# Strassen-Winograd weights on Trainium2: product P7's weights by subtraction from the running sum

## The chip, the cores and the metric

The kernel runs on one core of one Trainium2 chip. The metric is the device time of one execution in microseconds (us), the median of several runs. A profiled execution of the same program gives the page and the trace. In the trace PE is the matrix engine (TensorE), DVE is VectorE, ACT is ScalarE, POOL is GpSimd and SP is SyncE.

## The reference

One layer of a transformer-like block, batch 1, 512 tokens, width 2048, all in float32. A combined input projection feeds two token mixers, grouped-query attention and a Fourier mixing. Each is multiplied by a SiLU gate and projected to 2048 channels. The two are merged with sigmoid gates, and one output projection feeds a gated residual and a final norm:

```
g_a = sigmoid(p_rest[..., R_GA:R_GB]);  g_b = sigmoid(p_rest[..., R_GB:])
y_a = (attn * silu(z_a)) @ w_pa
y_b = (fourier_mix(u_b) * silu(z_b)) @ w_pb
return (g_a * y_a + g_b * y_b) @ w_o
```

The change touches how the weights of `g_a`, `g_b` (2048 x 4096 together) and `w_o` (2048 x 2048) are prepared.

## The kernel before

**Products.** These two products are computed in six groups: groups 0 to 3 for the gates, then the branch projections, then groups 4 and 5 for `w_o`. A group is a 2x2 block product in the form of Strassen and Winograd: seven products instead of eight. Each takes one form of the activations and one combination of the four weight blocks (0,0), (0,1), (1,0), (1,1). `PRODUCTS` (line 49 on) names them. P1 takes block (0,0); Q5 takes (0,0) + (0,1); Q6 adds (1,1) to that, and Q4 adds (1,0). P2 takes (1,0), Q3 takes (1,1), and P7 takes (0,1) + (1,1). The orders are `ONE_GROUP` (P1, Q5, P2, Q6, P7, Q3, Q4; groups 0 to 3 and 5) and `OUT_GROUP` (P1, P2, Q5, Q6, P7, Q3, Q4; group 4).

**Pieces.** Each product comes in four pieces, with a weight tile of 128x1024 (512 KB) each. A piece is multiplied by 12 matmuls of 128x512: two column tiles, two token tiles, and three passes each (`mm3`, lines 258 to 260: high part by high part, high by low, low by high). `split_from` (lines 133 and 134) makes the two parts of a weight tile: ScalarE copies the rounded high part `whi`, VectorE subtracts it to get the low part `wlo`.

**The running sum.** Four tiles R, one for each piece (`chain`), hold the sum that P1, Q5, Q6 and Q4 use one after the other. SyncE loads block (0,0) into R for P1 (line 172). In groups 0 to 3 Q5's block is loaded as a raw tile and added by VectorE (line 205). Every other block is added by an accumulating DMA from GpSimd's queue (line 214), issued in the order of the code right after the split of the stage before.

**Raw tiles.** Blocks that don't go into R are loaded by SyncE (line 169) into raw slots: eight in groups 0 to 3, six in groups 4 and 5. `x` and other inputs take the same slots. A load is issued in the order of `todo`, when a slot has come free. P7 takes two raw tiles for a piece, and VectorE adds them (line 205) before the split. `get` splits several pieces ahead of the one that is multiplied: five in groups 0 to 3, four in groups 4 and 5.

**Order.** All engines work through their instructions in the order that the build's scheduler has written. VectorE also makes the sums of the products (lines 830, 876, 1204, 1205 and others), ScalarE moves finished products and computes the sigmoids. After the last product the two token tiles of the last quarter are normalized and stored, one after the other (lines 1222 to 1261).

Of the kernel before, what the change touches and what calls it, by code (L numbers as in the profile page):

```python
# [13 lines left out]
ALU = mybir.AluOpType  # L14
# [29 lines left out]

FORMS = ("Z5", "S2", "S3", "S4")
CHAIN = ((0, 0), (0, 1), (1, 1), (1, 0))
PRODUCTS = (("P1", "A11", 0, "a"), ("Q5", "Z5", 1, "b"), ("P2", "A12", ((1, 0),), "a"), ("Q6", "S2", 2, "b"),
            ("P7", "S3", ((0, 1), (1, 1)), "c"), ("Q3", "S4", ((1, 1),), "b"), ("Q4", "A22", 3, "c"))  # L50
ONE_GROUP = ("P1", "Q5", "P2", "Q6", "P7", "Q3", "Q4")
OUT_GROUP = ("P1", "P2", "Q5", "Q6", "P7", "Q3", "Q4")

# [32 lines left out]
def block_kernel(ctx, tc, xT, ctxT, x, c_row, w_ss, w_gate, vecs, qkg, rope, dft_c, dft_s,  # L86
                 w_start, w_kv, w_m, w_g, w_pab, w_o, final_g, out):
    nc = tc.nc
# [8 lines left out]
    wp = sb("wp")  # L97
# [14 lines left out]
    def uid(s):  # L112
        cnt[0] += 1
        return f"{s}{cnt[0]}"
# [14 lines left out]
    def bank2():  # L129
        return ps.tile([P, 1024], F32, tag="b2", bufs=2, name=uid("pd"))  # L130

    def split_from(src, hi, lo):
        nc.scalar.activation(hi, src, ACT.Copy)  # L133
        nc.vector.tensor_tensor(lo, src, hi.bitcast(F32), op=ALU.subtract)  # L134
# [3 lines left out]
    chain, left = [], [0] * 4  # L138
    raw_pools, hl_pools = [(wp, RAW, "raw", RAW)], [wp] * HL

    class Piece:
# [1 line left out]

        def __init__(self, key, parts, cols, n, kind="wp", stage=None, pc=0, nxt=None, dst=None):
            self.key, self.parts, self.cols, self.n, self.kind = key, parts, cols, n, kind
            self.stage, self.pc, self.nxt, self.dst = stage, pc, nxt, dst
            self.raws, self.out, self.aside = [], None, False

    def stream(key, src, *a, **k):
        todo.append(Piece(key, src if isinstance(src, list) else [src], *a, **k))
# [37 lines left out]
    def hl_tiles():  # L190
        hl_pools.append(hl_pools.pop(0))
        pool = hl_pools[-1]
        if isinstance(pool, tuple):
            return [slot_tile(p, (1024,), F32R) for p in pool]
        if isinstance(pool, int):
            return [Halves([pairs[2 * pool + k][i][:, :, 256:] for k in range(2)]) for i in range(2)]
        return [pool.tile([P, 1024], F32R, tag=t, bufs=hl_pools.count(pool), name=uid("w" + t)) for t in ("hi", "lo")]

    def split_piece(e):
        if e.out is not None or e.kind == "raw":  # L200
            return
        raws = [r for _, r in e.raws]
        src = raws.pop(0) if e.stage is None else chain[e.pc]
        for r in raws:
            nc.vector.tensor_tensor(src, src, r, op=ALU.add)  # L205
        hi, lo = e.dst() if e.dst else hl_tiles()
        if isinstance(hi, Halves):
            for k in range(2):
                split_from(src[:, 512 * k : 512 * k + 512].rearrange("p (a c) -> p a c", a=2), hi.parts[k], lo.parts[k])
        else:  # L210
            hi, lo = hi[:, : e.cols], lo[:, : e.cols]
            split_from(src, hi, lo)
        if e.nxt is not None:
            nc.gpsimd.dma_start(src, e.nxt, accum_op=ALU.add)
        if e.stage == 3:
            left[e.pc] = 0
        r = lambda t: t if isinstance(t, Halves) else t.rearrange("p (n m) -> p n m", n=e.n)
        e.out = (r(hi), r(lo))

    def get(key):  # L220
        load_more()
        turn = [e for e in ahead if not e.aside]
        assert turn[0].key == key, (turn[0].key, key)
        for e in turn[: len(hl_pools)]:
            split_piece(e)
        load_more()
        e = turn[0]
        ahead.remove(e)
        free.extend(p[0::2] for p, _ in e.raws if p in retired)
        return e.raws[0][1] if e.kind == "raw" else e.out  # L230
# [12 lines left out]
    def slot_tile(p, shape, dt):  # L243
        return p[0].tile([P] + list(shape), dt, tag=p[1], bufs=1, name=uid("s"))
# [70 lines left out]
    def stream_product(name, g, w, by_dve):  # L315

        what = next(p[2] for p in PRODUCTS if p[0] == name)
        for pc in range(4):
            key = (name, g, pc)
            if isinstance(what, tuple):  # L320
                stream(key, [w[a, b, pc] for a, b in what], 1024, 2)
            else:
                part = lambda i: w[CHAIN[i][0], CHAIN[i][1], pc]
                stream(key, [part(what)] if what in by_dve else [], 1024, 2, stage=what, pc=pc,
                       nxt=part(what + 1) if what < 3 and what + 1 not in by_dve else None)
                todo[-1].first = part(0)

    flat = lambda v: v.rearrange("p t c -> p (t c)")
# [7 lines left out]
    for g in range(4):  # L336
        for name in ONE_GROUP:
            stream_product(name, g, w_g[g], BY_DVE_GATES)
            if g == 0 and name in LOADED:
                todo.extend(lambda f=f, h=h: load_form(f, h) for f in LOADED[name] for h in range(2))  # L340
            if g >= 2 and name in DONE:
                half, c = DONE[name]
                stream(("yb", half, 2 * (g % 2) + c), flat(yb_d[half, 2 * (g % 2) + c]), 1024, 2, "raw")
# [7 lines left out]
    for name in OUT_GROUP:  # L351
        stream_product(name, 4, w_o[1], BY_DVE_OUT)
        if name in DONE:
            half, c = DONE[name]
            stream(("x", half, 2 + c), flat(x[half, 2 + c]), 1024, 1, "raw")
    for name in ONE_GROUP:
        stream_product(name, 5, w_o[0], BY_DVE_OUT)
        half, c = {"P2": (0, 0), "P7": (1, 1), "Q3": (1, 0)}.get(name, (0, 0))
        if name == "Q3":
            stream(("x", 0, 1), flat(x[0, 1]), 1024, 1, "raw")  # L360
            todo.insert(len(todo) - 5, todo.pop())
        if name in ("P2", "P7", "Q3"):
            stream(("x", half, c), flat(x[half, c]), 1024, 1, "raw")
# [4 lines left out]
    part = ppool.tile([P, NS - 2, T], F32, name="part")  # L368
# [313 lines left out]
    for which, half in ((0, 0), (0, 1), (1, 1)):  # L682
        toks = range(3 * half, 3 * half + 3) if which == 0 else (4, 5)
        b = bank2()
        accs = [b[:, :512], b[:, 512:], bank()]
        for pc in range(8):
# [9 lines left out]
            if keys and pc in (1, 3, 5):  # L696
                a, t = keys.pop(0)
# [3 lines left out]
        for a, t in zip(accs, toks):  # L701
            a = a.rearrange("p (h d) -> p h d", h=4)
# [213 lines left out]
    def load_form(f, h, q=None):  # L916
        if (f, h) not in whole:
            return False
        i = FORMS.index(f)
        (q or nc.sync).dma_start(whole[f, h], f_d[i, :, 4 * h : 4 * h + 4, :])  # L920
# [128 lines left out]

    for i, f in enumerate(FORMS):  # L1050
        forms[f] = [None] * 8
# [33 lines left out]

    raws, merged, mf, comb = {}, {}, {n: [None] * 8 for n in ("A11", "A12", "A22") + FORMS}, {}
    held = {}
# [282 lines left out]
```

## Time and profile before

| | |
|---|---|
| median of 3 runs | 1386.93 us (1384.67 to 1387.5) |
| profiled execution | 1383.63 us |
| its span, first to last instruction | 1381.9 us |
| mean granted TensorE clock | 0.994 |
| PE busy | 1348.6 us (98%) |
| DVE, ACT, POOL busy | 911.2 us (66%), 629.7 us (46%), 113.7 us (8%) |
| HBM read | 257.34 MB |
| group 0 | from 757.4 us |
| groups 1, 2, 3 | from 839.4, 915.5, 991.7 us |
| branch projections | from 1067.8 us |
| groups 4, 5 | from 1204.4, 1284.7 us |
| last matmul | 1369.5 us |

A row of a timeline has the start in us from the start of the span, the duration in us, the engine, the line, the operation, output <- inputs by the program's names with buffer numbers left out, and in brackets the engine's idle time before it with what ended it. `wr` is a raw tile, `R` the running sum, `x` and `y` are accumulators of products. Busy time is an average over stages with different limits; what a change in one stage is worth is read from that stage.

### The profile page before, as it was taken

To read this page: it belongs to the slowest core of one execution; us is meant where nothing else is said; L and a number is where in the kernel's file an instruction comes from. 1 tells how busy PE (TensorE), PEld (TensorE's weight loads), DVE (VectorE), ACT (ScalarE), POOL (GpSimd) and SP (SyncE) were. 2 spreads that over 40 slices of the span, in tenths; PEclk is the share of its full clock that TensorE was granted. 3 is DMA by queue.
4 is the path that set the end of the run, shared out by engine and by line. 5 is a ranking of instruction groups with operands and counts; after the bars stand their busy time and mean duration, and the time that the engine had idled before them with its cause. 6 is when DMAs were issued, how large, how long until landed. Compare 5 with 4: busy or idle time off the path is not lost. (4 is left out here: it accounts for less than half of the span.)

```text
span 1381.9 us, 17609 instructions
## 1 busy us (share of the span) xinstructions
PE 1348.6 (98%) x6810; PEld 1105.2 (80%) x6810; DVE 911.2 (66%) x1191; ACT 629.7 (46%) x861; POOL 113.7 (8%) x167
## 2 busy tenths in 40 slices
PE   7999999999999999999999899999999999999986
PEld 4667789888888888888887688888888888878865
DVE  5765596767866658756743776665956546477577
ACT  5322253534545445455544655453544224364534
POOL 0110000011100001000000100100010100020100
PEclk9999999999999999999999999999999999999998
DMA  9887453635453334433446998888898854488973
GB/s 384 333 349 264 164 187 104 190 122 185 147 152 108 121 116 148 149 100 114 130 142 242 348 300 246 249 228 253 274 275 297 315 153 138 132 190 272 237 222 130
DMA packets 76115, 283.67 MB, mean 205 GB/s; under 512 B 8704, under 2 KB 9344, under 8 KB 71680
## 3 DMA queue, kind: packets, MB, share of 16 engines
q1 hardware_dynamic: 53712, 188.42, 40.6%
q0 software_dynamic: 17136, 76.56, 20.6%
q10 hardware_dynamic: 5184, 17.57, 3.3%
q8 instruction: 53, 0.87, 0.3%
q14 instruction: 30, 0.25, 0.1%
HBM read 257.34 MB, written 25.17 MB: 204 GB/s over the span
## 5 line engine op out<-in xcount | busy, mean ns | idle before, releaser
L133 ACT ACTIVATE whi<-wr 128x1024 fp32r<-128x1024 f32 x178 | 185.2, 1044 | 295.8 <-PE pb L259 83.6
L134 DVE TENSOR_TENSOR wlo<-wr,whi 128x1024 fp32r<-128x1024 f32 x178 | 213.7, 1204 | 143.2 <-ACT whi L133 143.0
L258 PE MATMUL pb<-s,whi 128*128 128x512 f32 x512 | 206.7, 405 | 1.3 <-ACT s L424 1.3
L259 PE MATMUL pb<-s,whi 128*128 128x512 f32 x512 | 200.7, 392 | 0.1
L260 PE MATMUL pb<-s,wlo 128*128 128x512 f32 x512 | 200.4, 392 | 0.0
L259 PE MATMUL y<-wlo,s 128*128 128x512 f32 x320 | 126.7, 396 | 7.1 <-DVE wlo L134 7.0
L259 PE MATMUL x<-wlo,s 128*128 128x512 f32 x324 | 126.7, 391 | 1.5 <-DVE wlo L134 1.5
L258 PE MATMUL x<-whi,s 128*128 128x512 f32 x324 | 126.7, 391 | 1.3 <-ACT s L836 1.1
L258 PE MATMUL y<-whi,s 128*128 128x512 f32 x320 | 126.1, 394 | 0.2 <-ACT s L833 0.2
L260 PE MATMUL x<-whi,s 128*128 128x512 f32 x324 | 126.3, 390 | 0.0
L260 PE MATMUL y<-whi,s 128*128 128x512 f32 x320 | 125.7, 393 | 0.0
L258 PEld LDWEIGHTS pb<-s,whi 128*128 128x128 f32 x512 | 96.1, 188 | 22.4 <-issue 3.7
L260 PEld LDWEIGHTS pb<-s,wlo 128*128 128x128 f32 x512 | 96.1, 188 | 21.1 <-issue 0.4
L259 PEld LDWEIGHTS pb<-s,whi 128*128 128x128 f32 x512 | 96.4, 188 | 17.1 <-DVE s L425 1.0
L133 ACT ACTIVATE whi<-R 128x1024 fp32r<-128x1024 f32 x66 | 69.7, 1059 | 64.6 <-PE x L260 39.4
L134 DVE TENSOR_TENSOR wlo<-R,whi 128x1024 fp32r<-128x1024 f32 x66 | 80.1, 1220 | 17.1 <-ACT whi L133 17.1
L973 ACT ACTIVATE p<-pd,mx 128x768 f32<-128x768 f32 x48 | 43.2, 899 | 87.3 <-DVE mx L971 87.3
L259 PEld LDWEIGHTS y<-wlo,s 128*128 128x128 f32 x320 | 60.7, 190 | 22.4 <-DVE wlo L134 9.9
L259 PEld LDWEIGHTS x<-wlo,s 128*128 128x128 f32 x324 | 60.8, 188 | 15.5 <-DVE wlo L134 3.1
L258 PEld LDWEIGHTS x<-whi,s 128*128 128x128 f32 x324 | 60.8, 188 | 14.7 <-ACT s L836 1.5
L258 PEld LDWEIGHTS y<-whi,s 128*128 128x128 f32 x320 | 60.7, 190 | 13.4 <-ACT s L833 0.5
L260 PEld LDWEIGHTS y<-whi,s 128*128 128x128 f32 x320 | 60.8, 190 | 12.7
(270 smaller groups left out, 2662.1 us busy)
## 6 DMA issues: line engine op xcount, KB each, us to landing
wr<-in_w_g SPq DMA_DIRECT2D x80, 512.0 KB, 7.9
wa<-in_w_ss POOLq DMA_DIRECT2D x28, 1024.0 KB, 8.2
wr<-in_w_m SPq DMA_DIRECT2D x44, 512.0 KB, 3.7
wr<-in_w_gate SPq DMA_DIRECT2D x32, 512.0 KB, 3.7
wr<-in_w_pab SPq DMA_DIRECT2D x32, 512.0 KB, 4.4
R<-in_w_g POOLq DMA_DIRECT2D x32, 512.0 KB, 9.6
wr<-in_w_o SPq DMA_DIRECT2D x32, 512.0 KB, 5.0
wr<-in_w_start SPq DMA_DIRECT2D x26, 512.0 KB, 7.1
```

The source lines that it names most:

```text
L133: nc.scalar.activation(hi, src, ACT.Copy)
L134: nc.vector.tensor_tensor(lo, src, hi.bitcast(F32), op=ALU.subtract)
L258: nc.tensor.matmul(o, ah, bh, start=start, stop=False, skip_group_check=cont)
L259: nc.tensor.matmul(o, ah, bl, start=False, stop=False, skip_group_check=cont)
L260: nc.tensor.matmul(o, al, bh, start=False, stop=stop, skip_group_check=cont)
L973: nc.scalar.activation(p, sc[:, :NKEY], ACT.Exp, bias=mx[:, 0:1], accum_out=mx[:, 1:2])
```

## The change

P7 now loads block (0,0) as its only raw tile, and VectorE subtracts it from the running sum of three: R - (0,0) = (0,1) + (1,1). The accumulation of the fourth block (1,0) into R was issued behind Q6's split. It is now issued behind P7's piece, because the subtract reads R as well. In all, 24 loads of 512 KB go; the number of VectorE instructions stays. In the changed file most lines stand one to four lines further down: the split is at 134 and 135, the gates' add at 206, the new subtract at 208, the loads at 170 and 173, the accumulating DMA at 217.

```diff
-            ("P7", "S3", ((0, 1), (1, 1)), "c"), ("Q3", "S4", ((1, 1),), "b"), ("Q4", "A22", 3, "c"))
+            ("P7", "S3", ((0, 0),), "c"), ("Q3", "S4", ((1, 1),), "b"), ("Q4", "A22", 3, "c"))
...
         for r in raws:
             nc.vector.tensor_tensor(src, src, r, op=ALU.add)
+        if e.off:
+            nc.vector.tensor_tensor(src, chain[e.pc], src, op=ALU.subtract)
         hi, lo = e.dst() if e.dst else hl_tiles()
...
         if e.nxt is not None:
-            nc.gpsimd.dma_start(src, e.nxt, accum_op=ALU.add)
+            nc.gpsimd.dma_start(chain[e.pc], e.nxt, accum_op=ALU.add)
...
+            part = lambda i: w[CHAIN[i][0], CHAIN[i][1], pc]
             if isinstance(what, tuple):
-                stream(key, [w[a, b, pc] for a, b in what], 1024, 2)
+                off = name == "P7"
+                stream(key, [w[a, b, pc] for a, b in what], 1024, 2, pc=pc, nxt=part(3) if off else None, off=off)
             else:
-                part = lambda i: w[CHAIN[i][0], CHAIN[i][1], pc]
                 stream(key, [part(what)] if what in by_dve else [], 1024, 2, stage=what, pc=pc,
-                       nxt=part(what + 1) if what < 3 and what + 1 not in by_dve else None)
+                       nxt=part(what + 1) if what < 2 and what + 1 not in by_dve else None)
```

More of the change, by code (lines that the diff above doesn't have):

```diff
@@ L141, in block_kernel, with __init__ @@
     class Piece:
-        def __init__(self, key, parts, cols, n, kind="wp", stage=None, pc=0, nxt=None, dst=None):
+        def __init__(self, key, parts, cols, n, kind="wp", stage=None, pc=0, nxt=None, dst=None, off=False):
             self.key, self.parts, self.cols, self.n, self.kind = key, parts, cols, n, kind
             self.stage, self.pc, self.nxt, self.dst = stage, pc, nxt, dst
-            self.raws, self.out, self.aside = [], None, False
+            self.raws, self.out, self.aside, self.off = [], None, False, off
     def stream(key, src, *a, **k):
```

## The prediction

> **What bounds the kernel now.** I read the page's head first, then the waits of TensorE, then the busy time by stage, then single rows of the timelines around the two places where TensorE stands still.
>
> ```profile
> span 1381.9 us, 17609 instructions
> PE 1348.6 (98%) x6810; PEld 1105.2 (80%) x6810; DVE 911.2 (66%) x1191; ACT 629.7 (46%) x861; POOL 113.7 (8%) x167
> PEclk9999999999999999999999999999999999999998
> ```
>
> TensorE is busy 98% of the span and its matmuls stay the same, so the change can only act on the few microseconds in which TensorE waits, on its clock, and on what follows its last matmul. The waits of TensorE name who is late (total, times, longest):
>
> ```profile
> PE y L259 <- DVE wlo L134: 7.0, 4, 4.5
> PE x L259 <- DVE wlo L134: 1.5, 3, 0.9
> ```
>
> L259 is the second of the three passes, the first that needs the low part `wlo`; it waits for VectorE's split. By stage (start:end, length, busy of each engine, then clock, DMA share, GB/s; group 0 of the gates, groups 1 and 3, the last product group, and the tail):
>
> ```profile
> core 0: us, PE busy (x) PEld busy (x) DVE busy (x) ACT busy (x) POOL busy (x), PEclk, DMA share, GB/s
> 757.40:839.40 82.00, 78.20 (x338) 62.56 (x338) 62.43 (x64) 46.90 (x56) 7.46 (x9) 1.00 0.97 313
> 839.40:915.50 76.10, 76.10 (x337) 63.02 (x336) 49.35 (x53) 38.37 (x46) 6.92 (x8) 1.00 0.85 250
> ...
> 991.70:1067.80 76.10, 76.10 (x337) 63.04 (x336) 53.48 (x56) 38.13 (x46) 6.92 (x8) 1.00 0.92 277
> ...
> 1284.70:1369.50 84.80, 80.07 (x337) 64.42 (x335) 59.68 (x61) 36.93 (x51) 8.58 (x10) 0.96 0.70 185
> 1369.50:1381.90 12.40, 0.39 (x2) 0.00 (x0) 5.29 (x15) 3.58 (x11) 0.00 (x0) 0.62 0.76 275
> ```
>
> Groups 1 and 3 have no idle TensorE at all. Group 0 loses 3.8 us with the DMA engines 97% busy, the last group 4.7 us, and only there the clock is below 1.00. The rows of TensorE (start, duration, instruction, idle before):
>
> ```profile
> 779.16 0.50 PE L259 MATMUL y<-wlo,s 128*128 128x512 f32 x1 [2.12 <-DVE wlo L134]
> ...
> 1339.46 0.80 PE L259 MATMUL y<-wlo,s 128*128 128x512 f32 x1 [4.46 <-DVE wlo L134]
> ...
> 1345.16 0.39 PE L260 MATMUL y<-whi,s 128*128 128x512 f32 x1
> ...
> 1346.08 0.40 PE L258 MATMUL y<-whi,s 128*128 128x512 f32 x1
> ...
> 1369.50 0.40 PE L260 MATMUL y<-whi,s 128*128 128x512 f32 x1
> ```
>
> The 4.46 us stand in P7 of the last group. Full rate is one matmul in 0.23 us (four starts from 1345.16 to 1346.08). From 1339.46 to 1345.16 thirteen starts took 5.70 us instead of 3.0: the clock was halved after the gap, another 2.7 us. The 2.12 us gap in group 0 had no such sequel.
>
> Why P7 is late there, from VectorE, the chain of waits and SyncE's queue:
>
> ```profile
> 1337.04 1.22 DVE L205 TENSOR_TENSOR wr<-wr,wr 128x1024 f32<-128x1024 f32 x1 [5.96 <-DMA wr<-in_w_o]
> 1338.18 1.22 DVE L134 TENSOR_TENSOR wlo<-wr,whi 128x1024 fp32r<-128x1024 f32 x1
> ...
> 1360.51 1.22 DVE L1204 TENSOR_TENSOR s<-x,s 128x1024 f32<-128x1024 f32 x1
> ...
> 1362.78 1.22 DVE L1205 TENSOR_TENSOR s<-s,s 128x1024 f32<-128x1024 f32 x1
> ...
> 1372.53 0.75 DVE L1250 TENSOR_TENSOR s<-y,s 128x256 f32<-128x256 f32 x2
> ...
> 1328.33 8.68 DMA wr<-in_w_o
> ...
> 1300.94 15.69 SPq L169 DMA_DIRECT2D wr<-in_w_o  x6
> ...
> 1327.20 1.46 SPq L169 DMA_DIRECT2D wr<-in_w_o  x2
> ```
>
> The add of the fourth piece of P7 (L205 at 1337.04) waits for its second raw block, which was issued only at 1328.33 (with six raw slots, a load waits for the split that frees one); the third piece's `wlo` (1338.18) stands behind it in VectorE's fixed order, and TensorE waits for that one.
>
> **Part 1, the last group: the second raw block goes.** P7 now loads four blocks instead of eight (24 loads fewer over six groups), and four slots come free with the four splits of P2, in the stretch of the x6 row, 1300.94 to 1316.6. With the 8.68 us that the slowest quoted load took all four are in by 1325.3. P7 starts at 1329.2 (25 matmuls of 0.23 and the gap before 1339.46). The add that waited 5.96 us becomes a subtract of equal size (1.22 us) that waits for nothing late. The 4.46 us gap and the 2.7 us of half clock go: −7.2. What is late next: the two other waits of the same row of TensorE's waits (7.0 − 4.46 − 2.12 = 0.4 in both) are left as they are. The running sum's third block is in before P7 too, since its accumulation was issued for Q6's split.
>
> The tail gains more than that. L1205 ran at 1362.78, because VectorE worked off the backlog from 1337.04 without a gap; L1204, which needs Q3's product, at 1360.51. Q3 ended about 1358.5 (48 matmuls of 0.23 before the end at 1369.50). Without backlog L1204, one split and L1205 run right behind Q3, that is L1205 2.3 us after Q3's end instead of 4.3: −2.0. The work between L1205 and L1250 at 1372.53 is a chain on VectorE and ScalarE; L1250 could come at most 2.5 us nearer to TensorE's end before it met it. Sum of part 1: −7.2 − 2.0 = −9.2.
>
> **Part 2, the gate groups: a subtract that waits.** The subtract needs the running sum with its third block; there an accumulating DMA from GpSimd's queue, issued only once Q5's split is done. In the order of the changed program the subtract for P7's first piece stands ahead of Q5's third `wlo` in group 0, the one for which TensorE already waits at 779.16:
>
> ```profile
> 774.48 3.49 DVE L134 TENSOR_TENSOR s<-s,s 128x1024 fp32r<-128x1024 f32 x3
> 777.89 2.35 DVE L134 TENSOR_TENSOR wlo<-R,whi 128x1024 fp32r<-128x1024 f32 x2
> ...
> 771.50 0.91 POOL L214 DMA_DIRECT2D R<-in_w_g  x1 [25.55 <-DVE wlo L134]
> ...
> DMA to landing us min/median/max: 8.3/8.3/8.3
> ...
> DMA to landing us min/median/max: 5.6/10.0/13.4
> ...
> DMA to landing us min/median/max: 3.6/8.1/14.4
> ```
>
> The landing rows are those of this one accumulation, of group 1's eight, and of all loads into R. It lands at 771.5 + 8.3 = 779.8. The new order has two of the three `s` splits, then the subtract, then `wlo`: VectorE is free at 774.48 + 2 × 1.135 = 776.75, waits to 779.85, subtracts to 780.98 and makes `wlo` from there instead of from 777.89: +3.1 us of gap, 5.2 us in all. Bounds: landing alone (5.6) would give 771.5 + 5.6 + 1.13 = 778.2, +0.3; landing as late as 14.4 gives 785.9, +9.2. I take 8.3: the same loads are in flight, since the slots that a P7 block gave up are filled by the next piece. Queued behind the subtract are Q5's third and fourth `wlo`; TensorE waits for the first of them.
>
> A 5.2 us gap is longer than the 4.46 us one that was followed by half clock, so I charge the same 2.7 us again. It may be spared, so 0 and 2.7 are the bounds. The Trainium skill (TensorE: Matmul & The Clock Gate, "What's actually happening") says that the clock halves after a free-running window of about 3.4 us without work. By that rule a 5.2 us gap holds a whole window in (5.2 − 3.4) / 3.4, about half of the cases, an estimate; the 4.46 us and the 2.12 us gap above agree with it. The Trainium skill (DMA: Bandwidth & Descriptors, "Anatomy of one DMA") puts a GpSimd DMA at 2.0 us plus bytes over 436 GB/s, which for 512 KB is 3.2 us, an estimate; by it the subtract would wait for nothing and the sum would be −9.2. The row has 8.3 us, and that decides.
>
> In groups 1 and 3 the subtracts also stand ahead of splits of Q5 and P2, and now also delay the issue of the next accumulations:
>
> ```profile
> 849.37 0.86 POOL L214 DMA_DIRECT2D R<-in_w_g  x1 [0.37 <-DVE s L134]
> ...
> 864.07 0.39 PE L259 MATMUL x<-wlo,s 128*128 128x512 f32 x1
> ...
> 1001.83 0.86 POOL L214 DMA_DIRECT2D R<-in_w_g  x1 [1.48 <-DVE s L134]
> ...
> DMA to landing us min/median/max: 11.1/11.1/11.1
> ...
> 1013.66 0.39 PE L259 MATMUL x<-wlo,s 128*128 128x512 f32 x1
> ```
>
> Group 1: the fourth accumulation, at 849.37 and 13.4 us long, lands at 862.8; subtract and split behind it end at 865.1, where TensorE wants `wlo` at 864.07: +1.0. But it was the fourth of four in a row; delayed by some 4 us it lands alone, 849.4 + 4 + 5.6 = 859, and nothing waits. Group 3: the third one lands at 1001.83 + 11.1 = 1012.9, `wlo` at 1015.2 against 1013.66: +1.5, or nothing by the same reasoning. I take 0 for both and keep +2.5. In groups 2 and 4 I charge nothing: the last subtract stands behind P2's splits there.
>
> **What costs nothing.** VectorE has as many instructions as before, a subtract for an add. The fourth block's accumulation is issued from GpSimd's queue once P7's subtract and Q6's split are done; its user Q4 comes two products after P7, 96 matmuls or 22 us, against 14.4 us for the slowest landing. If that cover were gone Q4 would wait. The 12 MB less traffic lie beside TensorE's work.
>
> **Sum.** −9.2 + 3.1 + 2.7 = −3.4. The profiled execution took 1383.63 us (1381.9 and 1.7 around), so 1380.2; the median of the runs is 3.3 above it, and the same difference gives 1383.5.
>
> **Rivals.** (1) *The clock is spared* in group 0, or the accumulation lands sooner there: −6.1 (no half clock) to −8.9 (landing alone), 1378.0 to 1380.8. For: the 2.12 us gap. Against: 4.46 us did trigger it. (2) *Groups 1 and 3 pay as well*: −3.4 + 2.5 = −0.9, 1386.0. For: up to 13.4 us of landing; against: 76.10 of 76.10 busy. (3) *Slower: accumulations bind the gate groups.* In group 0, where the DMA share is 0.97, the awaited landing goes from 8.3 to 14.4: +6.1, with rival 2's 2.5 that is −3.4 + 8.6 = +5.2, 1392.1. It breaks even at a landing of 9.2 us with rival 2 in force, 11.7 without. For: group 1's median of 10.0; against: this very load took 8.3. (4) *Slower: the end keeps its gap*, because P7's blocks or the running sum come late there too: then 3.1 + 2.7 = +5.8, 1392.7. Against: four slots for four blocks. (5) *Nothing moves*, the loads being hidden and the subtract's wait covered, or the change not doing what it says because the scheduler keeps the old waits: 1386.9. Against: the wait at 1337.04 is for a block that is no longer loaded.
>
> **Numbers.** Forecast 0.35, (1) 0.25, (2) 0.17, (3) 0.13, (4) 0.05, (5) 0.05. A measurement of this kernel can tell about 0.2%, 2.8 us, from no change. Faster by more: 0.35 + 0.25 = 0.60; within: 0.17 + 0.05 = 0.22; slower: 0.18. The range 1377.5 to 1387.5 holds the forecast, (1), (2) and (5), and leaves out (3) and (4).
>
> **What would show it.** Right: no add or subtract of the last group waits for `in_w_o`, P7 there takes 10.9 us at full clock, L1205 runs 2.3 us behind Q3; in group 0 the subtract waits for `R<-in_w_g` until about 779.8, and TensorE's gap before Q5's third piece is about 5.2 us, with half clock behind it. Wrong: a gap of more than 1 us in group 1 or 3, or a gap left in the last P7.

## The result and the profile after

The changed kernel takes 1380.92 us (median of 4 runs, 1379.43 to 1381.71) against 1387.22 us before (4 runs): a ratio of 0.9958 with a 95% interval of 0.9946 to 0.9971, or −5.8 us (7.5 to 4.0). The forecast was −3.4 us and 1383.5, with a range from 1377.5 to 1387.5: the range holds the measured time, while −3.4 lies just outside the interval of the measured difference. The profiled execution took 1381.71 us, its span 1379.9 us. This is only 1.9 us less than the 1383.63 us of before; the first profiled execution of before turned out shorter than any of that kernel's other runs in this pair, and experiment 4 shows why that matters.

The stages of the two traces, cut at the starts of the products (before, then after; start:end, length, busy of each engine, clock, DMA share, GB/s). They are group 0, groups 1 to 3, the branch projections, groups 4 and 5 up to P7 of group 5, this P7, and the rest:

```profile
757.44:839.36 81.92, 78.12 (x338) 62.52 (x336) 62.39 (x64) 46.90 (x56) 7.46 (x9) 1.00 0.97 313
839.36:1067.84 228.48, 228.48 (x1010) 189.19 (x1008) 153.69 (x161) 112.20 (x136) 20.71 (x24) 1.00 0.89 262
1067.84:1204.36 136.52, 136.29 (x626) 112.99 (x624) 68.00 (x58) 43.71 (x49) 10.19 (x18) 1.00 0.58 187
1204.36:1329.17 124.81, 123.21 (x545) 100.58 (x544) 91.52 (x79) 63.41 (x78) 18.93 (x22) 1.00 0.89 229
1329.17:1347.45 18.28, 13.82 (x49) 10.86 (x48) 12.32 (x12) 5.53 (x6) 0.00 (x0) 0.81 0.75 229
1347.45:1381.90 34.45, 22.44 (x97) 17.75 (x95) 25.19 (x41) 14.92 (x31) 0.00 (x0) 0.86 0.35 129
```
```profile
757.97:845.70 87.73, 79.92 (x337) 64.24 (x336) 63.23 (x64) 47.88 (x56) 7.45 (x9) 0.96 0.86 268
845.70:1074.24 228.54, 228.54 (x1009) 189.16 (x1008) 153.39 (x160) 111.90 (x135) 20.71 (x24) 1.00 0.84 232
1074.24:1210.24 136.00, 136.00 (x625) 113.07 (x624) 69.30 (x59) 44.99 (x50) 10.19 (x18) 1.00 0.59 192
1210.24:1334.30 124.06, 122.73 (x545) 100.64 (x544) 95.14 (x82) 64.75 (x79) 18.93 (x22) 1.00 0.84 204
1334.30:1345.18 10.88, 10.88 (x49) 9.01 (x48) 8.73 (x8) 4.25 (x4) 0.00 (x0) 1.00 0.80 281
1345.18:1379.90 34.72, 22.54 (x97) 17.76 (x95) 25.52 (x42) 14.80 (x31) 0.00 (x0) 0.89 0.39 136
```

Group 0 is 5.8 us longer and its clock falls to 0.96. Groups 1 to 3 are unchanged, with no idle TensorE. The last P7 is 7.4 us shorter, at full clock. The rest gains nothing: 34.45 us before, 34.72 after. In group 0 (TensorE, VectorE, GpSimd, and the landing of that accumulation):

```profile
783.84 0.79 PE L262 MATMUL y<-wlo,s 128*128 128x512 f32 x1 [5.32 <-DVE wlo L135]
...
788.57 0.40 PE L261 MATMUL y<-whi,s 128*128 128x512 f32 x1
```
```profile
775.59 2.35 DVE L135 TENSOR_TENSOR s<-s,s 128x1024 fp32r<-128x1024 f32 x2
781.42 1.23 DVE L208 TENSOR_TENSOR wr<-R,wr 128x1024 f32<-128x1024 f32 x1 [3.48 <-DMA R<-in_w_g]
782.57 2.35 DVE L135 TENSOR_TENSOR wlo<-R,whi 128x1024 fp32r<-128x1024 f32 x2
```
```profile
773.03 0.91 POOL L217 DMA_DIRECT2D R<-in_w_g  x1 [26.55 <-DVE wlo L135]
...
DMA to landing us min/median/max: 8.4/8.4/8.4
```

The accumulation is issued at 773.03 and lands 8.4 us later. The subtract (L208) waits 3.48 us for it, and the `wlo` for which TensorE waits comes behind it. Eleven starts from 783.84 to 788.57 take 4.73 us instead of 2.5: the clock is halved, 2.2 us. In the last group VectorE reads:

```profile
1314.87 1.23 DVE L208 TENSOR_TENSOR wr<-R,wr 128x1024 f32<-128x1024 f32 x1 [5.34 <-DMA wr<-in_w_o]
...
1324.43 1.23 DVE L208 TENSOR_TENSOR wr<-R,wr 128x1024 f32<-128x1024 f32 x1
...
1330.12 1.22 DVE L135 TENSOR_TENSOR wlo<-wr,whi 128x1024 fp32r<-128x1024 f32 x1
```

All four subtracts are done by 1325.7, ahead of P7's start at 1334.3. The first three still wait for their blocks (5.34, 1.09 and 0.32 us), but at a place where TensorE has work in store.

### The profile page after: what moved, and what is told of

Same layout as the page of the kernel before. It is cut to its first block, busy times and chain, and to the rows that moved or that the text cites. A ratio compares the mean times of both kernels' runs of the same rounds, so it can differ in the third digit from the quotient of the medians.

```text
span 1379.9 us, 17559 instructions
## 1 busy us (share of the span) xinstructions
PE 1347.1 (98%) x6810; PEld 1105.2 (80%) x6810; DVE 913.3 (66%) x1191; ACT 632.2 (46%) x861; POOL 113.7 (8%) x167
## 5 line engine op out<-in xcount | busy, mean ns | idle before, releaser
L261 PEld LDWEIGHTS x<-whi,s 128*128 128x128 f32 x324 | 60.8, 188 | 15.3 <-ACT s L840 1.5
L261 PEld LDWEIGHTS y<-whi,s 128*128 128x128 f32 x320 | 60.6, 189 | 13.3 <-ACT s L837 0.5
L263 PEld LDWEIGHTS x<-whi,s 128*128 128x128 f32 x324 | 60.8, 188 | 12.6
```

Source lines behind the costliest of these rows:

```text
L261: nc.tensor.matmul(o, ah, bh, start=start, stop=False, skip_group_check=cont)
L263: nc.tensor.matmul(o, al, bh, start=False, stop=stop, skip_group_check=cont)
```

## Experiments

Each kernel was timed against the kernel before on the same chip; the ratio in brackets is the 95% interval, and a us figure is the ratio's distance from 1 times about 1386. The first set restricts the subtraction to some groups; the edit is one tuple, with the other groups as before:

```diff
+SUB = (4, 5)
...
+        sub = g in SUB
+        if name == "P7" and not sub:
+            what = ((0, 1), (1, 1))
...
-                off = name == "P7"
+                off = name == "P7" and sub
...
-                       nxt=part(what + 1) if what < 2 and what + 1 not in by_dve else None)
+                       nxt=part(what + 1) if what < (2 if sub else 3) and what + 1 not in by_dve else None)
```

**1. Groups 4 and 5 only.** Expected:

> The subtraction only in groups 4 and 5; groups 0 to 3 load two blocks for P7 as before. Theory (the gain is the gap in the last P7, the loss is the subtract that waits in group 0): the last P7 takes 10.9 us at full clock, group 0 has its old gap of about 2 us and no half clock, and the time is 5 to 6 us below the changed kernel, about 1375. Rival (the gain is the lighter traffic in the gate groups): most of the gain is lost, about 1384 to 1387.

Measured: 1378.11 us, 0.9946 (0.993 to 0.9963), −7.5 us. Most of the gain is in these groups, and the rival fails. In the trace group 0's gap is 1.73 us, at full clock, and the last P7 has no gap. It did not come down to 1375.

**2. Groups 0 to 3 only** (`SUB = (0, 1, 2, 3)`). Expected:

> The subtraction only in groups 0 to 3; groups 4 and 5 load two blocks for P7 as before. Theory: group 0 has a gap of about 5.3 us with half clock behind it, the last P7 has its gap of about 4.5 us with half clock, and the time is 5 to 6 us above before, about 1393. Rival (lighter traffic): below before, 1381 to 1384.

Measured: 1388.11 us, 1.0015 (1.0004 to 1.0025), +2.1 us. The sign is as expected, the amount less than half of it: something in these groups gains. TensorE's waits show both gaps (5.4 is group 0's; the last P7's is 3.8):

```profile
PE y L263 <- DVE wlo L136: 9.8, 3, 5.4
```

**3. All groups but group 0** (`SUB = (1, 2, 3, 4, 5)`). Expected:

> The subtraction in groups 1 to 5, group 0 as before. Theory: as with groups 4 and 5 alone, about 1375, since groups 1 to 3 had no idle matrix engine before and have none after. If waits in groups 1 and 3 cost what my upper bound said, it is up to 2.5 us above that; if lighter traffic in groups 1 to 3 helps, it is below it.

Measured: 1375.72 us, 0.993 (0.9914 to 0.9946), −9.7 us. This is the fastest version that leaves nothing out, ahead of both kernels. Group 0 has about its old gap (1.71 us here, 2.12 before), and the clock stays full:

```profile
781.23 0.50 PE L263 MATMUL y<-wlo,s 128*128 128x512 f32 x1 [1.71 <-DVE wlo L136]
```

**4. The kernel before, a second trace.** No edit. Expected:

> The kernel before, unchanged, for a second trace: its first profiled execution took 1383.63 us, the other runs 1384.67 to 1388.29. If the spread comes from the gaps that stand in the first trace, this one shows a longer gap in group 0 or in the last P7 when it is slower; rival: the spread lies elsewhere, spread over many stages.

Measured: 1387.94 us, span 1386.2 us, 4.3 us above the first trace. Most of the surplus stands where neither theory had put it, in the branch projections (139.71 us from their first matmul to the first of group 4, where the first trace has 136.52). The waits at their start, and that of the last P7:

```profile
1070.08 0.50 PE L259 MATMUL y<-wlo,s 128*128 128x512 f32 x1 [0.68 <-DVE wlo L134]
...
1082.25 0.50 PE L258 MATMUL y<-whi,s 128*128 128x512 f32 x1 [1.22 <-ACT whi L133]
...
1083.70 0.50 PE L259 MATMUL y<-wlo,s 128*128 128x512 f32 x1 [0.95 <-DVE wlo L134]
...
1343.79 0.80 PE L259 MATMUL y<-wlo,s 128*128 128x512 f32 x1 [4.89 <-DVE wlo L134]
```

The first three waits sum to 2.85 us; in the first trace the same place has one of 0.23. ScalarE waits there for the attention output, `at_d`, which SyncE loads into raw tiles:

```profile
ACT s L133 <- DMA wr<-at_d: 12.4, 4, 5.4
```

SyncE issues the first of these six loads at 1046.09 in this trace and at 1040.27 in that of experiment 3, where group 3 has four loads fewer in the queue ahead of it. The five behind it come there at about the same time or later, though, the last one 5 us later (this trace, then experiment 3):

```profile
1070.06 0.83 SPq L169 DMA_DIRECT2D wr<-at_d  x1
```
```profile
1075.23 0.33 SPq L171 DMA_DIRECT2D wr<-at_d  x1
```

What differs is the order in which the build wrote ScalarE's instructions. Here the split for which TensorE waits at 1082.25 (`whi` at 1081.16) stands behind the split of the sixth `at_d` block; in experiment 3 the same `whi` stands ahead of it and runs at 1076.88. All six traces with the old form in groups 1 to 3 have the first order, all eight with the subtraction the second (this trace, then experiment 3):

```profile
1080.19 1.06 ACT L133 ACTIVATE s<-wr 128x1024 fp32r<-128x1024 f32 x1 [2.75 <-DMA wr<-at_d]
1081.16 1.04 ACT L133 ACTIVATE whi<-wr 128x1024 fp32r<-128x1024 f32 x1
```
```profile
1076.88 1.05 ACT L135 ACTIVATE whi<-wr 128x1024 fp32r<-128x1024 f32 x1
...
1081.01 1.06 ACT L135 ACTIVATE s<-wr 128x1024 fp32r<-128x1024 f32 x1 [0.55 <-DMA wr<-at_d]
```

**5. Group 0 only** (`SUB = (0,)`). Expected:

> The subtraction only in group 0. Theory: the wait ahead of Q5's third split costs the gap's growth (2.1 to 5.3 us) and a half clock of 2 to 3 us, so 4 to 6 us above before; the gap in the last P7 stays. Rival (four loads fewer help the most crowded stage): no difference or faster.

Measured: 1391.89 us, 1.0039 (1.0025 to 1.0053), +5.4 us, as expected. The gap is there, followed by half clock:

```profile
782.63 0.80 PE L263 MATMUL y<-wlo,s 128*128 128x512 f32 x1 [5.52 <-DVE wlo L136]
```

**6. Groups 1 to 3 only** (`SUB = (1, 2, 3)`). Expected:

> The subtraction only in groups 1 to 3. Theory: two traces with the old form there show waits of 0.9 to 2.9 us at the start of the branch projections, two traces with the subtraction show none, so 1 to 3 us below before. Rival: those waits come and go by themselves, and the time is that of before within 1 us; should the subtracts wait as my upper bound said, it is up to 2.5 us above.

Measured: 1383.07 us, 0.9974 (0.9964 to 0.9985), −3.6 us. The gain is there, a little over the forecast. This run's profiled execution (1383.56 us) is as long as the first one of before (1383.63), whose trace had almost no waits there. TensorE has no wait of over 0.15 us from 1060 to 1090 in any of the eight traces that have the subtraction in these groups. Of the six without it, five have waits there that sum to 0.2 to 2.9 us (before twice, experiments 1, 5 and 7), and one has none (experiment 9).

**7. Group 5 only** (`SUB = (5,)`). Expected:

> The subtraction only in group 5. Theory: the whole gain of the last P7, gap and half clock, 6 to 8 us below before, as with groups 4 and 5 together. Rival (half of that gain comes from group 4): 3 to 4 us below.

Measured: 1378.64 us, 0.9941 (0.9928 to 0.9953), −8.2 us. Group 4 adds nothing that the times can tell.

**8. The residual's instructions on GpSimd**, on top of experiment 3. Expected:

> Group 0 as before, the subtraction in groups 1 to 5, and the four VectorE instructions that add the residual to two output quarters ahead of Q3 and Q4 of the last group go to GpSimd. Theory (the tail was not shortened because VectorE works without a gap from Q3's first split to the last sum, backlog or not): 4.5 us of VectorE's work less, the last sum runs closer to Q3's end and the time is 1.5 to 2.5 us below that of the same kernel without this edit, about 1373.5. Rival (the tail is the chain behind the last matmul): no difference.

```diff
-        nc.vector.tensor_tensor(t, t, row(gates, j), op=ALU.mult)
-        nc.vector.tensor_tensor(t, get_x(half, j), t, op=ALU.subtract)
+        nc.gpsimd.tensor_tensor(t, t, row(gates, j), op=ALU.mult)
+        nc.gpsimd.tensor_tensor(t, get_x(half, j), t, op=ALU.subtract)
```

Measured: 1377.07 us, 0.9933 (0.992 to 0.9946): no difference from experiment 3. This does not decide the question, because VectorE was not relieved:

```profile
1331.07 3.42 DVE L838 TENSOR_TENSOR s<-s,s 128x1024 f32<-128x1024 f32 x1
...
1337.75 3.42 DVE L136 TENSOR_TENSOR s<-wr,s 128x1024 fp32r<-128x1024 f32 x1
```
```profile
1330.10 3.30 POOL L1205 TENSOR_TENSOR s<-s,s 128x1024 f32<-128x1024 f32 x1 [6.11 <-DVE s L838]
...
1336.71 3.39 POOL L1205 TENSOR_TENSOR s<-s,s 128x1024 f32<-128x1024 f32 x1
```

While GpSimd worked on its four instructions, four of VectorE that otherwise take 1.22 us took 3.19 to 3.42.

**9. Both blocks of P7, but free slots**, from the kernel before. Expected:

> The kernel before, with both blocks of P7 loaded, but in group 5 the four blocks of the residual input are not loaded, and the instructions that add them use a resident tile instead, so that their raw slots are free. The residual of the first 1024 columns is left out. Theory (the last P7 was late because its last block could not be issued before a slot came free): eight blocks have six slots instead of four, the last one is issued ahead of Q6's split, the gap and the half clock go, and the time is 6 to 9 us below before. Rival (the blocks are late because eight of them take too long to move): the gap stays, 0 to 2 us below.

```diff
     def get_x(half, j):
+        if j < 2:
+            return row(gates, j)
...
-        if name in ("P2", "P7", "Q3"):
-            stream(("x", half, c), flat(x[half, c]), 1024, 1, "raw")
```

(The load of the fourth residual block goes in the same way.) Measured: 1380.38 us, 0.9965 (0.9952 to 0.9978), −4.9 us, less than expected (the two medians are 6.3 us apart). In the trace P7 has its eight blocks and its adds, and one wait of 0.50 us in place of 4.46:

```profile
1327.69 0.50 PE L259 MATMUL y<-wlo,s 128*128 128x512 f32 x1 [0.50 <-DVE wlo L134]
```

P7's last block is now issued well ahead of P7's start at 1326.81; before, it was issued at 1328.33, 0.8 us ahead of the start at 1329.17:

```profile
1318.95 0.33 SPq L169 DMA_DIRECT2D wr<-in_w_o  x1
```

So the gap goes with the late issue, and eight blocks for P7 are not too many. The edit also takes four loads of the residual out of this group; it does not tell a free slot from a shorter queue. The profiled execution took 1374.99 us, though, and the four others 1380.3 to 1383.08. Their mean clock of 0.996 to 0.997 gives no sign of more half clock than in the trace (0.996). The waits at the branch projections, which this trace does not have, cost up to 3.7 us in others; whether they account for part of the 5 to 8 us is open.

**10. The residual's instructions left out**, on top of experiment 3. Expected:

> Group 0 as before, the subtraction in groups 1 to 5, and the four VectorE instructions that add the residual to two output quarters ahead of Q3 and Q4 of the last group are left out, so these two quarters lack their residual and its gate. Theory (VectorE's work in the last two products sets the tail): the last sum comes up to 2.5 us earlier against TensorE's last matmul, and the time is 2 to 3 us below the kernel with the subtraction in groups 1 to 5, about 1373. Rival (the tail is the chain behind the last matmul): no difference.

```diff
-        nc.vector.tensor_tensor(t, t, row(gates, j), op=ALU.mult)
-        nc.vector.tensor_tensor(t, get_x(half, j), t, op=ALU.subtract)
+        get_x(half, j)
```

Measured: 1378.0 us, 0.9942 (0.9928 to 0.9955): no gain. It says nothing on VectorE's work, since the loads moved as well, probably because the edit also took away what frees the residual's slot early. SyncE issued Q3's later loads 3.2 to 5.6 us later than in experiment 3. ScalarE waited for them, and VectorE for ScalarE:

```profile
1342.77 1.23 DVE L136 TENSOR_TENSOR s<-wr,s 128x1024 fp32r<-128x1024 f32 x1 [4.07 <-ACT s L135]
```

**11. The changed kernel, a second time.** No edit. Expected:

> The changed kernel, unchanged, for a second trace and for times beside the others. If the parts add up, it is 4 to 6 us above the kernel with the subtraction in groups 1 to 5, and about 6 us below before; the gap in group 0 is again 5 to 5.5 us with half clock, and no wait stands at the start of the branch projections.

Measured: 1380.91 us, 0.9966 (0.9953 to 0.9979), −4.7 us. Group 0's gap is 5.15 us with half clock, and no wait stands at the start of the branch projections. By the two ratios it is 0.36%, or 5 us, above experiment 3.

**12. The same instructions, narrow**, on top of experiment 3. Expected:

> Group 0 as before, the subtraction in groups 1 to 5, and the four VectorE instructions ahead of Q3 and Q4 of the last group work on 64 columns instead of 1024, so that every wait and slot stays and only their time (about 1 us each) goes; these two quarters lack most of their residual and its gate. Theory (VectorE works without a gap from Q3's first split to the last sum, and that sets the tail): the last sum comes 2 to 2.8 us earlier against the last matmul, and the time is 1.5 to 2.8 us below the kernel with the subtraction in groups 1 to 5. Rival (the tail is the chain behind the last matmul): no difference.

```diff
+        c = (slice(None), slice(None), slice(0, 32))
-        nc.vector.tensor_tensor(t, t, row(gates, j), op=ALU.mult)
-        nc.vector.tensor_tensor(t, get_x(half, j), t, op=ALU.subtract)
+        nc.vector.tensor_tensor(t[c], t[c], row(gates, j)[c], op=ALU.mult)
+        nc.vector.tensor_tensor(t[c], get_x(half, j)[c], t[c], op=ALU.subtract)
```

Measured: 1375.63 us, 0.9928 (0.9914 to 0.9942), no difference from experiment 3 that the times can tell. The trace moves the way that the theory said, by less than half of the 2 to 2.8 us expected (experiment 3, then this one; the last sum, and TensorE's last matmul):

```profile
1357.23 1.22 DVE L1213 TENSOR_TENSOR s<-s,s 128x1024 f32<-128x1024 f32 x1
...
1363.95 0.40 PE L264 MATMUL y<-whi,s 128*128 128x512 f32 x1
```
```profile
1354.41 1.22 DVE L1214 TENSOR_TENSOR s<-s,s 128x1024 f32<-128x1024 f32 x1
...
1362.03 0.40 PE L264 MATMUL y<-whi,s 128*128 128x512 f32 x1
```

The last sum stands 6.7 us ahead of the last matmul in the one and 7.6 us in the other. From the last matmul to the end of the span it is 12.15 us (1376.1 − 1363.95) and 11.27 us (1373.3 − 1362.03). In the thirteen other traces it is 12.1 to 12.4 us. So VectorE's work does set part of the tail, 0.9 us; that the time falls by it is not shown.

## Why the prediction was right, and where it was not

The direction and the two large terms are shown, by experiments that hold one of them each. The parts add up within their uncertainty of some 2 us each: +5.4 (group 0) − 3.6 (groups 1 to 3) − 8.2 (group 5) = −6.4, beside −5.8 and −4.7 measured for the whole. Beside group 5, groups 1 to 3 gave less than alone: experiment 3 (−9.7) is 1.5 us below experiment 7 and 2.2 below experiment 1, which is about the uncertainty.

- **The last P7, forecast −7.2.** Right: −7.40 in the traces (18.28 to 10.88), and −8.2 by experiment 7. The cause named, a second block that is issued late because it waits for a slot, is borne out by experiment 9 as far as the late issue goes. That the subtract "waits for nothing late" is true only of P7's own time: the sign named for it, that no subtract of the last group waits for `in_w_o`, did not show, as the 5.34 us at 1314.87 say.
- **Group 0, forecast +3.1 of gap and +2.7 of half clock.** Right: the gap grew from 2.12 to 5.32 us (+3.2), half clock cost 2.2, and experiment 5 has +5.4. The landing of 8.3 us, carried over from before, came out at 8.4. The two ends of the bounds (5.6 and 14.4) were not needed. Charging the half clock in full was right; the share of about half of the cases that the prediction worked out beside it was too low, since all nine gaps of 3.80 to 5.52 us in the fourteen traces were followed by half clock.
- **Groups 1 and 3, forecast 0 with +2.5 as a bound.** Right: 228.48 and 228.54 us for groups 1 to 3, all of them busy. Rivals 2 and 3 fail. Rival 1 (1378.0 to 1380.8) lies nearer to the measured 1380.92 than the forecast, and fails all the same: the half clock and the landing of 8.4 us are in the trace.
- **The tail, forecast −2.0.** Wrong. From the last matmul's start to the end of the span it is 12.4 us before (1381.9 − 1369.5) and 12.3 after (1379.9 − 1367.56). The step that failed is the one that put L1205's delay down to the backlog of 1337.04. The trace of before already had a gap of 0.61 us on VectorE at 1357.09, so the work behind 1337.04 was not without a gap. In the changed kernel VectorE is late without that backlog (before; then ScalarE and VectorE after):

```profile
1357.09 1.22 DVE L134 TENSOR_TENSOR s<-R,s 128x1024 fp32r<-128x1024 f32 x1 [0.61 <-ACT s L133]
```
```profile
1340.83 1.06 ACT L134 ACTIVATE whi<-wr 128x1024 fp32r<-128x1024 f32 x1 [5.26 <-DMA wr<-in_w_o]
```
```profile
1341.92 1.23 DVE L135 TENSOR_TENSOR wlo<-wr,whi 128x1024 fp32r<-128x1024 f32 x1 [2.15 <-ACT whi L134]
...
1355.16 1.23 DVE L135 TENSOR_TENSOR s<-R,s 128x1024 fp32r<-128x1024 f32 x1 [0.60 <-ACT s L134]
...
1358.58 1.21 DVE L1208 TENSOR_TENSOR s<-x,s 128x1024 f32<-128x1024 f32 x1
...
1360.84 1.22 DVE L1209 TENSOR_TENSOR s<-s,s 128x1024 f32<-128x1024 f32 x1
```

  Q3 ends at 1356.2, and L1209 (L1205 before) starts 4.6 us behind it, where 2.3 had been forecast and 4.3 stood before. VectorE first waits 2.15 us for the split of Q3's first piece, for whose block ScalarE waits (it was issued at 1331.36 and took 9.4 us to land). From there to L1209 it has 18 instructions with the same gap of 0.6 us between them, and from that gap to the last sum it is 5.7 us in both traces. By these rows, what holds VectorE back is Q3's late block and the work behind it, not the backlog that the prediction named; experiment 12 shows 0.9 us of the tail for part of that work.
- **The branch projections, forecast 0.** The term was missing. In the six traces with the old form in groups 1 to 3 this stage takes 136.00 to 139.71 us, in the eight with the subtraction 136.00 each time. By the times it is worth 3.6 us (experiment 6), or 1.5 to 2.2 (experiment 3 against 7 and 1). It is not that the loads of `at_d` come earlier: only the first does. In the traces ScalarE's splits stand in another order, and a `whi` that TensorE needs no longer stands behind the last `at_d` block. That this order is what removes the waits is read from the traces; it was not tried alone, and why the build chose it stays open. The prediction had looked at the queues only where the trace of before showed a wait, and that trace had almost none here (0.23 us). One profiled execution was a poor sample of a wait that varies from run to run.

The measured −5.8 against −3.4 is then the missing term (−1.5 to −3.6) and the tail (+2.0), of opposite signs, and small differences in the two large terms. That the total came out as near as it did is in part luck: two errors took each other off.

## What to carry to other kernels

Ahead of a subtract or add that takes the place of a load, look at where the scheduler puts it: in an engine that works in order, an instruction that waits for a DMA holds up every one behind it. Here the same edit gave 8.2 us where its operands were early and cost 5.4 us where they were not, so apply it stage by stage; leaving out group 0 made the kernel 9.7 us faster than before rather than 5.8. Leaving out loads also changed the order that the build wrote for a stage further on. So read the stages behind the edit too; a second trace of the unchanged kernel shows which waits come and go.

## What the runs showed of the hardware

In experiment 8 GpSimd's four two-input instructions of 128x1024 float32 took 2.76 to 3.39 us, and VectorE's beside them 3.19 to 3.42 instead of 1.22. The ends fit two engines that take turns, one holding the other up for the whole instruction: GpSimd's work from 1336.71 ends at 1340.10, and VectorE's from 1337.75 ends at 1341.17, 1.07 us later. In the same way each of GpSimd's four ends 2.25 to 2.27 us after the VectorE instruction that ran when it started, so some 2.3 us is its own time, an estimate from these rows, and the rest is waiting. The Trainium skill (SBUF — State Buffer, "Terms") says that VectorE and GpSimd share a pair of ports with a lock for the whole instruction; the trace agrees.

All nine gaps of TensorE from 3.80 to 5.52 us in the last P7 and in group 0 were followed by half clock, which cost 1.7 to 2.7 us each; single gaps of up to 2.12 us there were not. A long gap is not needed, though. In group 0 of experiment 6 half clock came after two gaps of 1.26 and 0.94 us with one matmul between them (a start every 0.43 us instead of 0.23, seen in the duration of 0.63), and in experiment 8 after two of 0.80 and 0.95 us:

```profile
762.26 0.50 PE L262 MATMUL x<-whi,s 128*128 128x512 f32 x1 [1.26 <-ACT whi L135]
763.71 0.50 PE L263 MATMUL x<-wlo,s 128*128 128x512 f32 x1 [0.94 <-DVE wlo L136]
...
764.67 0.63 PE L263 MATMUL x<-wlo,s 128*128 128x512 f32 x1
```

Two gaps of 1.22 and 0.95 us at 1082.25 and 1083.70 in experiment 4 were not followed by it. So in these traces a gap of 3.8 us or more was enough each time, and for shorter ones the length alone does not tell. The rule of a whole window without work, from which the prediction worked out its half of the cases, does not fit experiments 6 and 8.
